# Encoder layer in Strassen-Winograd steps: weight-operand splits moved between VectorE and GpSimd, down-weight sums taken singly, change-overs of the down-projection lengthened

## The chip, the cores and the metric

The kernel runs on one core of one Trainium2 chip. The metric is device time in microseconds (us), from the first to the last instruction of an execution with what lies around it. The core's engines are TensorE (PE: matmuls, PEld: weight loads), VectorE (DVE), ScalarE (ACT), GpSimd (POOL) and SyncE (SP), which here only issues DMAs. Each engine takes its instructions in the order in which they are written; between engines they wait for semaphores.

## What is computed

One layer of a bidirectional encoder, in float32, on 2048 + 1024 tokens of width 1024, with the same weights. First token mixing (input projection, Fourier groups, gating heads, output projection), then channel mixing, of which this text treats:

```
def _channel_mixer(h, w_up, conv_w, conv_b, w_down):
    a = h @ w_up                                   # 1024 -> 2 * 2816
    ap = jnp.pad(a, ((0, 0), (1, 1), (0, 0)))
    a = ap[:, :-2] * conv_w[0] + ap[:, 1:-1] * conv_w[1] + ap[:, 2:] * conv_w[2] + conv_b
    gate, up = a[..., :D_FF], a[..., D_FF:]        # D_FF = 2816
    return (jax.nn.gelu(gate) * up) @ w_down
```

RMSNorm stands before and after each half, and a residual is added.

## The kernel before

**Split products.** A float32 matmul is made of three in a faster format: each operand is split into h (a rounded copy, made by ScalarE) and l (the rest, source minus h, a subtraction of two SBUF tiles of 128x512 by VectorE or GpSimd), and h*h, h*l and l*h are summed in PSUM. `split` (L99) does this for the moving weights of a step, `Stage.prep` (L148) for the operands that stay through a stage.

**Steps and products.** The large projections run as Strassen-Winograd steps: a 2x2 block product done in seven smaller products, from sums of the operands. Class `Step` holds one: `sums` makes four sums of the left operand on GpSimd (s0 to s3 in the profile, L181 to L184), `prep(j)` splits left operand j (tiles w0 to w6), `mm(j)` is one product: 3n matmuls of 128x512, n = 4 in the up-projection, and 3 or 4 in the down-projection. `post(j)` combines the results out of PSUM on VectorE. The seven products are named B11, B21, T4, T2, T3, T1, B22 (indices 0 to 6), and p0 to p6 in the profile are their results.

**Slots.** The order of all work is written out by hand. `at(slot, order, fn)` notes a function for a slot; slots are counted in products of TensorE, and within a slot LOAD comes before PREP, MM, OUT and STORE. At the end all is written in this order. Left operands are split LEAD slots ahead of their product (3 in up-projection blocks 1 and 2, otherwise 2) and loaded 6 slots ahead.

**Up-projection.** Three blocks of 1024 tokens; in each, 22 steps (ft) of seven products. The stage operands x (7 times 4 tiles) stay through a block; `turnover` spreads the loading and splitting of the next block's over slots around the block boundary: it starts `lead` slots before it and spreads 28 tiles over `span` slots. The first two and last two steps of a block run as interleaved pairs. Of a step's seven splits the tuple `POOL` names those that GpSimd makes: (4,), T3 alone (tile w4u). After the products come the convolution (ACT, then VectorE in `taps`), GELU on ACT, and a multiply of 128x1024 on GpSimd (`gate`, L1190, t0u). Block 0 also computes the four sums per step and stores them; blocks 1 and 2 load them (tiles a0 to a6 of the half pool H).

**Down weights.** In block 1 also the four sums of the down-projection's weights are made, for 11 pairs of rows: `wd_load` (four loads), `wd_sums` (four subtractions and sums on GpSimd, L126 to L128 and L694), `wd_store` (four stores), once in 7 slots. They come behind a step's multiply.

**Down-projection.** Three groups q of the inner dimension, n = 3, 4 and 4; in each, 12 steps (tp) of seven products. The stage operands w (weights and their sums, tiles srw, split into sow) stay through a group, and `turnover` changes them with lead 10 and span 14 for q = 0, 6 and 10 for q = 1 and 2. In `Stage.prep` the tiles with even k are split by VectorE, those with odd k by GpSimd.

Of the kernel before, what the change touches and what calls it, by code (L numbers as in the profile page):

```python
# [15 lines left out]
ALU = mybir.AluOpType  # L16
# [17 lines left out]
def tile_trunk(  # L34
# [6 lines left out]
    nc = tc.nc  # L41
# [8 lines left out]
    def half(name, dt=F32, shape=(128, 512)):  # L50
        return H.tile(list(shape), dt, tag="h", name=name)
# [30 lines left out]
    vec = nc.vector  # L82
# [32 lines left out]
    LOAD, PREP, MM, OUT, STORE = range(5)  # L115

    def at(slot, order, fn, *args):
        events[slot].append((order, len(events[slot]), fn, args))
# [3 lines left out]
    B11, B21, T4, T2, T3, T1, B22 = range(7)  # L122

    def right_sums(t1, b11, b12, b21, b22, last=True):

        nc.gpsimd.tensor_tensor(t1, b12, b11, op=ALU.subtract)  # L126
        nc.gpsimd.tensor_tensor(b12, b22, b12, op=ALU.subtract)
        nc.gpsimd.tensor_tensor(b11, b12, b11, op=ALU.add)  # L128
        if last:
            nc.gpsimd.tensor_tensor(b21, b11, b21, op=ALU.subtract)  # L130


    class Stage:
# [14 lines left out]
        def prep(self, j, ks=range(4)):  # L148
            for k in ks:
                if k >= self.n:  # L150
                    return
                r = self.raw[j][k]
                t = unit(f"so{self.name}{j}{k}", F32R, (128, 2, 512))
                nc.scalar.copy(t[:, 0], r)
                eng = vec if k % 2 == 0 or self.name == 'x0' and j in (B11, T2) else nc.gpsimd
                eng.tensor_tensor(t[:, 1], r, t[:, 0].bitcast(F32), op=ALU.subtract)  # L156
                self.raw[j][k] = None
                self.op[j] = (self.op[j] or []) + [t]
# [429 lines left out]
    for pr in range(12):  # L588
        s = SB + 7 * pr
# [97 lines left out]
            nc.sync.dma_start(bs[q], wd[(ka, kb)[q // 2], :, c : c + 512])  # L687
        raws["wd", i] = bs

    def wd_sums(i):  # L690
        t1 = half(f"wt{i}")
        bs = raws["wd", i]
        right_sums(t1, *bs, False)
        nc.gpsimd.tensor_tensor(bs[2], bs[2], bs[0], op=ALU.subtract)  # L694
        bs.append(t1)

    def wd_store(i):
        b11, b12, b21, _, t1 = raws.pop(("wd", i))
# [322 lines left out]
    for i, m in enumerate(mixes):  # L1021
        s = B1 + 4 * i
# [55 lines left out]
    class Up(Step):  # L1078
# [5 lines left out]
        def __init__(self, stage, blk, ft):  # L1084
            super().__init__(stage, f"u{blk}_{ft}")
            self.blk, self.ft, self.t, self.src = blk, ft, {}, {}
            self.LEAD = 3 if blk else 2

        def fetch(self):
            for i in range(2):  # L1090
# [112 lines left out]
    s = B1 + 4 * len(mixes)  # L1203
    for blk in range(3):

        def x_src(j, a, m, dst, blk=blk):
            nc.sync.dma_start(dst[:, :m], xo_d[blk, j, :, a : a + m])

        stage = Stage(f"x{blk}", 4, x_src)
        if blk == 1:  # L1210
            for i in range(NFT // 2):
                at(s + 7 * i + 22, LOAD, wd_load, i)
                at(s + 7 * i + 25, PREP, wd_sums, i)
                at(s + 7 * i + 29, STORE, wd_store, i)
        if blk:
            turnover(s, stage, Up.ORDER, 12, 22)
        else:
            for i, j in enumerate(Up.ORDER):
                d = s + max(2 * i - 3, -2)
                at(d - 1 - (i > 0), LOAD, stage.load, j)  # L1220
                at(d, PREP - 0.3, stage.prep, j)
        for ft in range(NFT):
            u = Up(stage, blk, ft)

            pair = ft < 2 or ft > NFT - 3
            place(s - 7 * (ft % 2) if pair else s, u, ft % 2 if pair else None)
            first = blk == 0 and ft < 2
            if first:
                u.POOL = ()
                at(u.s0 - 2, LOAD, u.load)  # L1230
                at(u.s0 - 2, PREP - 0.2, u.sums)
                products(u)
            elif blk == 0:
                steps(u, 3)
            else:
                for i, j in enumerate(u.ORDER):
                    at(pos(u, i) - 6, LOAD, u.load_left, j)
                products(u)
            if blk == 0:
                at(u.s0 + (4 if pair else 2), STORE, u.sstore)  # L1240
            at(pos(u, 4), OUT + 0.1, u.centre, 1)
            at(pos(u, 4) + 1, OUT + 0.2, u.taps, 1, 0)
            at(pos(u, 4) + 2, OUT + 0.2, u.taps, 1, 1)
            at(pos(u, 6), OUT + 0.1, u.centre, 0)
            at(pos(u, 7), OUT + 0.2, u.taps, 0, 0)
            at(pos(u, 8), OUT + 0.6, u.taps, 0, 1)
            at(pos(u, 10), OUT + 0.3, u.gate)
            at(pos(u, 12), STORE, u.store)
            s += 7
        if blk == 1:  # L1250
            at(s + 5, OUT + 0.5, last_token)
            at(s + 6, STORE, last_token_store)
# [106 lines left out]
    for q in range(3):  # L1359

        def w_src(j, a, m, dst, q=q):
            k0, n = GROUPS[q]
            kk = KPAIRS.index((k0, k0 + n)) + a
            if j in (B11, B21, B22):
                k = k0 + a + (0 if j == B11 else n)
                c = 512 if j == B22 else 0
                src = wd[k : k + m, :, c : c + 512]
            else:
                src = wo_d[(T1, T2, T3, T4).index(j), kk : kk + m]
            nc.sync.dma_start(dst[:, :m], src.rearrange("k p n -> p k n"))  # L1370

        stage = Stage(f"w{q}", GROUPS[q][1], w_src)
        turnover(s, stage, Down.ORDER, *(() if q else (10, 14)))
        if q == 2:
            at(s - 2, LOAD, po_load)
        for tp in range(12):
            d = Down(stage, q, tp)
            place(s, d)
            steps(d, 3)
            if q == 0:  # L1380
                at(s + 8, STORE, d.cstore)
                s += 7
                continue
            at(s - 2, LOAD, d.cload)
            if q == 1:
                at(s + 8, STORE, d.cstore2, 0)
                at(s + 8, STORE, d.cstore2, 1)
            elif tp == 11:
                at(s + 1, LOAD, d.closing_load)
                at(s + 2, OUT + 0.1, d.square, 0, 0)  # L1390
                at(s + 4, OUT + 0.1, d.square, 1, 1)
                at(s + 5, OUT + 0.1, d.square, 0, 1)
                at(s + 6, OUT + 0.1, d.square, 1, 0)
                at(s + 6, OUT + 0.2, d.closing_out)
            else:
                e = 3 if d.closing else 0
                at(s + 10 - e, MM, d.squares)
                at(s + 11 - e, LOAD, d.xload)
                at(s + 11 - e, PREP + 0.5, d.scale)
                at(s + 12 - e, PREP + 0.5, d.yout, 1)  # L1400
                at(s + 14 - e, OUT + 0.3, d.yout, 0)
                at(s + 14 - e, STORE, d.ystore, 1)
                at(s + 15 - e, STORE, d.ystore, 0)
            s += 7
# [121 lines left out]
```

## Time and profile before

| | us |
|---|---|
| median of 3 runs (2756.62 to 2758.92) | 2758.53 |
| the profiled execution | 2759.55 |
| its span, first to last instruction | 2757.6 |
| PE busy | 2650.9 (96%) |
| DVE busy | 2156.4 (78%) |
| ACT busy | 1199.7 (44%) |
| POOL busy | 1172.1 (43%) |

The granted clock of TensorE is 0.986 of full speed on average. A busy time says how long an engine had an instruction in work; it includes time in which the instruction itself was held up. Idle time of an engine other than TensorE costs nothing as long as TensorE does not wait for it.

### The profile page before, as it was taken

What the parts mean: (1) busy time and instruction counts of PE and PEld (TensorE: products, weight loads), DVE (VectorE), ACT (ScalarE), POOL (GpSimd) and SP (SyncE); (2) the same over time, 40 slices, a digit from 0 to 9 for tenths busy, and PEclk for the clock granted to TensorE, in tenths of its full rate; (3) what the DMA queues carried; (4) which work ended last, traced back from release to release, by engine and by line L of the source; (5) the groups of instructions that cost most, each with busy time, mean ns of one, the idle gap of its engine ahead of it and who ended that gap; (6) DMA issues with size and microseconds to landing.
All of it is one profiled execution on the core that took longest, in us unless ns stands there. A gap on an engine that the chain in (4) does not pass through costs nothing.

```text
span 2757.6 us, 35060 instructions
## 1 busy us (share of the span) xinstructions
PE 2650.9 (96%) x11930; PEld 2164.6 (78%) x11930; DVE 2156.4 (78%) x3282; ACT 1199.7 (44%) x2261; POOL 1172.1 (43%) x772
## 2 busy tenths in 40 slices
PE   8899999999889999999999998999998999999998
PEld 7788877887768888877777886888886877887886
DVE  6777756678888788888888888888887567668887
ACT  5445524555544444454333444444444352224333
POOL 3644221235655556643444233222124344326666
PEclk9999999999999999999999999999999999999999
DMA  9223375658934445564665364343353475456665
GB/s 350 104 84 115 122 276 203 228 175 282 334 134 155 155 155 180 180 209 148 217 220 198 129 221 123 107 138 124 117 181 129 131 234 167 160 184 229 206 222 198
DMA packets 323923, 498.08 MB, mean 181 GB/s; under 512 B 27232, under 2 KB 176224, under 8 KB 323744
## 3 DMA queue, kind: packets, MB, share of 16 engines
q1 hardware_dynamic: 323744, 495.85, 54.3%
q8 instruction: 93, 1.52, 0.2%
q14 instruction: 86, 0.70, 0.1%
HBM read 337.42 MB, written 158.35 MB: 180 GB/s over the span
## 4 chain that ended last, share of the span: by engine, by line
PE 43%; DVE 7%; issue 3%; ACT 1%; DMA 1%; POOL 0%; SPq 0%; DVEq 0%; ACTq 0%; POOLq 0%
PE p0d L203 12%; PE p5u L203 4%; PE p4u L203 4%; PE p2u L203 4%; PE p3u L203 4%; PE p6d L203 3%; PE p0u L203 3%; PE p1d L203 3%; PE p5d L203 3%; PE p1u L203 3%; PE p6u L203 2%; DVE sow L156 1%; DVE w3u L101 1%; DVE t1u L1153 1%; DVE t0u L1153 1%
## 5 line engine op out<-in xcount | busy, mean ns | idle before, releaser
L1190 POOL TENSOR_TENSOR t0u<-t0u,t1u 128x1024 f32<-128x1024 f32 x66 | 177.3, 2688 | 424.7 <-ACT t0u L1189 267.2
L203 PE MATMUL p0u<-sox,w0u 128*128 128x512 f32 x792 | 194.6, 394 | 11.7 <-DVE w0u L101 11.6
L203 PE MATMUL p1u<-sox,w1u 128*128 128x512 f32 x792 | 194.3, 392 | 6.8 <-DVE w1u L101 6.6
L203 PE MATMUL p3u<-sox,w3u 128*128 128x512 f32 x792 | 195.2, 393 | 5.7 <-DVE w3u L101 4.9
L203 PE MATMUL p5u<-sox,w5u 128*128 128x512 f32 x792 | 194.0, 392 | 6.2 <-DVE w5u L101 6.2
L203 PE MATMUL p4u<-sox,w4u 128*128 128x512 f32 x792 | 192.7, 392 | 5.5 <-POOL w4u L101 5.0
L203 PE MATMUL p2u<-sox,w2u 128*128 128x512 f32 x792 | 191.9, 392 | 5.1 <-DVE w2u L101 5.1
L203 PE MATMUL p6u<-sox,w6u 128*128 128x512 f32 x792 | 191.1, 391 | 1.2 <-DVE w6u L101 1.2
L203 PEld LDWEIGHTS p0u<-sox,w0u 128*128 128x128 f32 x792 | 149.1, 189 | 47.3 <-DVE w0u L101 16.3
L1141 ACT ACTIVATE t1u<-p2u,cbt,cwt 128x512 f32<-128x512 f32 x66 | 51.5, 780 | 301.1 <-DVE p2u L1129 293.3
L203 PEld LDWEIGHTS p1u<-sox,w1u 128*128 128x128 f32 x792 | 147.2, 188 | 44.3 <-DVE w1u L101 13.3
L203 PEld LDWEIGHTS p3u<-sox,w3u 128*128 128x128 f32 x792 | 146.8, 188 | 43.9 <-DVE w3u L101 11.9
L203 PEld LDWEIGHTS p5u<-sox,w5u 128*128 128x128 f32 x792 | 146.6, 188 | 43.9 <-DVE w5u L101 12.8
L203 PEld LDWEIGHTS p4u<-sox,w4u 128*128 128x128 f32 x792 | 147.1, 188 | 42.5 <-POOL w4u L101 8.5
L203 PEld LDWEIGHTS p2u<-sox,w2u 128*128 128x128 f32 x792 | 149.8, 189 | 37.2 <-DVE w2u L101 5.9
L203 PEld LDWEIGHTS p6u<-sox,w6u 128*128 128x128 f32 x792 | 148.9, 188 | 33.9 <-DVE w6u L101 2.8
L1141 ACT ACTIVATE t0u<-p1u,cbt,cwt 128x512 f32<-128x512 f32 x66 | 51.5, 780 | 256.8 <-DVE p1u L1135 256.8
L1189 ACT ACTIVATE t0u<-t0u 128x1024 f32<-128x1024 f32 x66 | 70.1, 1062 | 171.2 <-DVE t0u L1153 139.3
L181 POOL TENSOR_TENSOR s0d<-ra1d 128x512 f32<-128x512 f32 (+1 forms) x36 | 50.2, 1396 | 204.1 <-DMA ra1d<-g_d 190.1
L93 POOL TENSOR_SCALAR r_v<-ss 128x2 f32<-128x2 f32 (+1 forms) x38 | 15.9, 417 | 261.4 <-ACT scr L894 156.7
L101 POOL TENSOR_TENSOR w4u<-a4u,w4u 128x512 fp32r<-128x512 f32 x44 | 61.3, 1395 | 143.6 <-ACT w4u L100 119.9
L1153 DVE SCALAR_TENSOR_TENSOR t0u<-p6u,cwt,t0u 128x511 f32<-128x511 f32 (+4 forms) x220 | 111.9, 534 | 7.1 <-ACT t0u L1141 2.0
(348 smaller groups left out, 7040.5 us busy)
## 6 DMA issues: line engine op xcount, KB each, us to landing
g_d<-t0u SPq DMA_DIRECT2D x66, 512.0 KB, 2.9
srx<-xo_d SPq DMA_DIRECT2D x42, 512.0 KB, 6.5
xT<-xT SPq DMA_DIRECT2D x24, 512.0 KB, 8.1
xc<-xc SPq DMA_DIRECT2D x24, 512.0 KB, 5.3
zz<-z_d SPq DMA_DIRECT2D x48, 256.0 KB, 5.8
xr<-x_po SPq DMA_DIRECT2D x24, 512.0 KB, 4.9
xo_d<-hT SPq DMA_DIRECT2D x48, 256.0 KB, 3.6
ra0d<-g_d SPq DMA_DIRECT2D x24, 512.0 KB, 4.6
```

The lines of the kernel that those rows point to most:

```text
L93: nc.gpsimd.tensor_scalar(v, ss, 1.0 / n, EPS, op0=ALU.mult, op1=ALU.add)
L101: (eng or vec).tensor_tensor(l, src, h.bitcast(F32), op=ALU.subtract)
L156: eng.tensor_tensor(t[:, 1], r, t[:, 0].bitcast(F32), op=ALU.subtract)
L181: nc.gpsimd.tensor_tensor(s1, a21, a22, op=ALU.add)
L203: nc.tensor.matmul(ps, lhsT=w[:, a, k], rhs=op[k][:, b], start=k == 0 and a + b == 0 and not chained, stop=k == n - 1 and a == 1, skip_gro ...
L1141: nc.scalar.activation(t[:, i], p, AF.Identity, bias=cbt[:, ti : ti + 1], scale=cwt[:, ti, 1:2])
L1153: vec.scalar_tensor_tensor(d, a, w, d, op0=ALU.mult, op1=ALU.add)
L1189: nc.scalar.activation(ga, ga, AF.Gelu_apprx_tanh)
L1190: nc.gpsimd.tensor_tensor(ga, ga, self.t[1], op=ALU.mult)
```

## The change

Four edits:

1. `Stage.prep`: the stage operands w of the down-projection are all split by VectorE (77 splits instead of 42; GpSimd made 35).
2. `wd_sums(i, n)` makes one of the four sums; they stand two slots apart, and a pair of rows comes every 12 slots instead of 7, from slot 10 of block 1 on instead of 22. The store is two slots behind the last sum.
3. In blocks 1 and 2 of the up-projection GpSimd makes three splits of a step, T3, T4 and B21 (w4u, w2u, w1u), instead of T3 alone.
4. The change-overs of the down-projection: lead and span (10, 14) become (14, 18) for q = 0, (6, 10) become (16, 20) for q = 1 and (7, 11) for q = 2.

```diff
-                eng = vec if k % 2 == 0 or self.name == 'x0' and j in (B11, T2) else nc.gpsimd
+                eng = vec if k % 2 == 0 or self.name[0] == 'w' or self.name == 'x0' and j in (B11, T2) else nc.gpsimd
...
-    def wd_sums(i):
-        t1 = half(f"wt{i}")
+    def wd_sums(i, n):
+
         bs = raws["wd", i]
-        right_sums(t1, *bs, False)
-        nc.gpsimd.tensor_tensor(bs[2], bs[2], bs[0], op=ALU.subtract)
-        bs.append(t1)
+        if n == 0:
+            bs.append(half(f"wt{i}"))
+        b11, b12, b21, b22, t1 = bs
+        out, x, y, op = (
+            (t1, b12, b11, ALU.subtract), (b12, b22, b12, ALU.subtract),
+            (b11, b12, b11, ALU.add), (b21, b21, b11, ALU.subtract),
+        )[n]
+        nc.gpsimd.tensor_tensor(out, x, y, op=op)
...
             self.LEAD = 3 if blk else 2
+            if blk:
+                self.POOL = (T3, T4, B21)
...
-                at(s + 7 * i + 22, LOAD, wd_load, i)
-                at(s + 7 * i + 25, PREP, wd_sums, i)
-                at(s + 7 * i + 29, STORE, wd_store, i)
+                d = s + 10 + 12 * i
+                at(d, LOAD, wd_load, i)
+                for n in range(4):
+                    at(d + 3 + 2 * n, PREP, wd_sums, i, n)
+                at(d + 11, STORE, wd_store, i)
...
-        turnover(s, stage, Down.ORDER, *(() if q else (10, 14)))
+        turnover(s, stage, Down.ORDER, *((14, 18), (16, 20), (7, 11))[q])
```

GpSimd's queue in block 1, from the multiply of step 7 on (t0u1_7; w4u1_9 is a split for step 9, wt and wd are sums of down weights). Before:

```order
L1190 TENSOR_TENSOR t0u1_7_12204<-t0u1_7_12204,t1u1_7_12158 128x1024
L126 TENSOR_TENSOR wt5_12315<-wd51_12236,wd50_12235 128x512
L127 TENSOR_TENSOR wd51_12236<-wd53_12238,wd51_12236 128x512
L128 TENSOR_TENSOR wd50_12235<-wd51_12236,wd50_12235 128x512
L694 TENSOR_TENSOR wd52_12237<-wd52_12237,wd50_12235 128x512
L101 TENSOR_TENSOR w4u1_9_12366<-a4u1_9_12291,w4u1_9_12366 128x512
L1190 TENSOR_TENSOR t0u1_8_12383<-t0u1_8_12383,t1u1_8_12337 128x1024
```

The same place now:

```order
L1197 TENSOR_TENSOR t0u1_7_12187<-t0u1_7_12187,t1u1_7_12140 128x1024
L700 TENSOR_TENSOR wt4_12320<-wd41_12247,wd40_12246 128x512
L101 TENSOR_TENSOR w4u1_9_12346<-a4u1_9_12274,w4u1_9_12346 128x512
L700 TENSOR_TENSOR wd41_12247<-wd43_12249,wd41_12247 128x512
L101 TENSOR_TENSOR w2u1_9_12397<-a2u1_9_12318,w2u1_9_12397 128x512
L700 TENSOR_TENSOR wd40_12246<-wd41_12247,wd40_12246 128x512
L101 TENSOR_TENSOR w1u1_9_12442<-a1u1_9_12370,w1u1_9_12442 128x512
L1197 TENSOR_TENSOR t0u1_8_12363<-t0u1_8_12363,t1u1_8_12315 128x1024
L700 TENSOR_TENSOR wd42_12248<-wd42_12248,wd40_12246 128x512
```

The burst of four sums behind the multiply is taken apart; two splits more stand between two multiplies.

VectorE's queue towards the end of group 0 of the down-projection, where the splits of group 1's stage operands begin (sow100: group 1, product B11, tile 0; w5d0_11: step 11 of group 0). Before:

```order
L101 TENSOR_TENSOR w5d0_11_19754<-s0d0_11_19672,w5d0_11_19754 128x384
L156 TENSOR_TENSOR sow100_19757<-srw100_19695,sow100_19757 128x512
L156 TENSOR_TENSOR sow102_19763<-srw102_19697,sow102_19763 128x512
L1307 TENSOR_TENSOR c0d0_11_19746<-c0d0_11_19746,p1d0_11_19766 128x512
L101 TENSOR_TENSOR w4d0_11_19783<-s2d0_11_19674,w4d0_11_19783 128x384
L156 TENSOR_TENSOR sow110_19789<-srw110_19713,sow110_19789 128x512
L101 TENSOR_TENSOR w6d0_11_19810<-s3d0_11_19675,w6d0_11_19810 128x384
L156 TENSOR_TENSOR sow112_19813<-srw112_19729,sow112_19813 128x512
```

Now:

```order
L156 TENSOR_TENSOR sow100_19588<-srw100_19528,sow100_19588 128x512
L156 TENSOR_TENSOR sow101_19591<-srw100_19528,sow101_19591 128x512
L1316 TENSOR_TENSOR c1d0_9_19542<-c1d0_9_19542,p6d0_9_19594 128x512
L101 TENSOR_TENSOR w1d0_10_19607<-ra0d0_10_19506,w1d0_10_19607 128x384
L156 TENSOR_TENSOR sow102_19610<-srw102_19544,sow102_19610 128x512
L101 TENSOR_TENSOR w3d0_10_19626<-s1d0_10_19563,w3d0_10_19626 128x384
L156 TENSOR_TENSOR sow103_19629<-srw102_19544,sow103_19629 128x512
L156 TENSOR_TENSOR sow110_19632<-srw110_19560,sow110_19632 128x512
```

They begin more than a step earlier, and tiles 1 and 3, GpSimd's before, stand in VectorE's queue. At the boundary from the up-projection, ahead of the first split w0d0_0, VectorE's queue holds 15 stage splits of group 0 where it held 8, and the splits w2u and w1u of the last two steps are gone from there.

## Rows read from the trace of the kernel before

**Rows 1.** Page, part 1: busy us, share of the span, instructions of TensorE

```profile
PE 2650.9 (96%) x11930; PEld 2164.6 (78%) x11930; DVE 2156.4 (78%) x3282; ACT 1199.7 (44%) x2261; POOL 1172.1 (43%) x772
```

**Rows 2.** Chain of waits: start us, length us, engine, result, line, matmuls

```profile
1269.86 2.72 PE p0u L203 x12
...
1294.50 2.72 PE p4u L203 x12
...
1502.16 2.72 PE p4u L203 x12
...
1633.07 5.45 PE p2u L203 x24
...
1737.99 2.72 PE p0u L203 x12
...
2042.63 5.44 PE p0u L203 x24
...
2120.49 4.08 PE p0d L203 x18
...
2249.01 4.09 PE p0d L203 x18
...
2295.27 5.44 PE p0d L203 x24
...
2485.67 5.45 PE p0d L203 x24
...
2533.74 5.44 PE p0d L203 x24
```

**Rows 3.** Timeline of TensorE, block 0's last pair: start us, length us, matmuls

```profile
1197.64 3.76 PE L203 MATMUL p1u<-sox,w1u 128*128 128x512 f32 x14
```

**Rows 4.** Windows: start:end, length; busy us (instructions): PE, PEld, DVE, ACT, POOL

```profile
1315.28:1336.06 20.78, 19.95 (x85) 15.45 (x85) 18.05 (x30) 8.05 (x13) 10.11 (x6) 1.00 0.68 215
1757.03:1776.07 19.04, 19.04 (x86) 15.77 (x85) 16.50 (x33) 8.20 (x14) 4.10 (x2) 1.00 0.38 126
2120.49:2134.77 14.28, 14.28 (x64) 11.82 (x64) 7.16 (x12) 5.24 (x11) 4.74 (x5) 1.00 0.41 129
2333.35:2352.39 19.04, 19.04 (x86) 15.77 (x85) 11.99 (x16) 4.36 (x7) 5.81 (x5) 1.00 0.50 165
2571.82:2590.86 19.04, 19.04 (x85) 15.77 (x85) 15.85 (x18) 6.46 (x11) 12.37 (x8) 1.00 0.69 220
```

**Rows 5.** Timelines of GpSimd and VectorE, block 1 (1345) and block 2 (1770)

```profile
1345.02 2.39 POOL L1190 TENSOR_TENSOR t0u<-t0u,t1u 128x1024 f32<-128x1024 f32 x1 [10.43 <-ACT t0u L1189]
...
1345.21 2.75 DVE L101 TENSOR_TENSOR w1u<-a1u,w1u 128x512 fp32r<-128x512 f32 x1
...
1770.98 0.68 DVE L101 TENSOR_TENSOR w1u<-a1u,w1u 128x512 fp32r<-128x512 f32 x1
```

**Rows 6.** Groups by line: busy us, mean ns of one, idle before and its releaser

```profile
L101 POOL TENSOR_TENSOR w4u<-a4u,w4u 128x512 fp32r<-128x512 f32 x44 | 61.3, 1395 | 143.6 <-ACT w4u L100 119.9 <-PE p3u L203 13.1 <-PE p0u L203 10.6
L156 DVE TENSOR_TENSOR sow<-srw,sow 128x512 fp32r<-128x512 f32 x42 | 58.9, 1415 | 0.3 <-ACT sow L154 0.3
L101 DVE TENSOR_TENSOR w1u<-a1u,w1u 128x512 fp32r<-128x512 f32 x44 | 54.6, 1241 | 9.0 <-ACT w1u L100 4.5 <-issue 4.3
```

**Rows 7.** Waits of TensorE (us, times, longest): block 1; first down step; whole span

```profile
PE p3u L203 <- DVE w3u L101: 4.9, 10, 0.5
...
PE p0d L203 <- DVE w0d L101: 3.9, 1, 3.9
...
PE p4u L203 <- POOL w4u L101: 5.0, 8, 0.6
```

**Rows 8.** Timelines of GpSimd and VectorE, change-over from group 0 to 1

```profile
2267.98 16.90 POOL L156 TENSOR_TENSOR sow<-srw,sow 128x512 fp32r<-128x512 f32 x10
...
2272.47 1.18 DVE L101 TENSOR_TENSOR w1d<-ra0d,w1d 128x512 fp32r<-128x512 f32 x1
2273.57 3.48 DVE L156 TENSOR_TENSOR sow<-srw,sow 128x512 fp32r<-128x512 f32 x2
```

## The prediction

> **What bounds the kernel now.** Read part 1 of the page first: TensorE is busy in 2650.9 us [rows 1], so a gain can come only out of the remainder and out of stretches where its products run at half clock or wait. Next the chain of waits. It is nearly all matmuls, and the start times of products show where the pace is lost. A product of the up-projection is twelve matmuls and takes 2.72 us [rows 2]; seven make a step of 19.04 us, which block 2 and the second group of the down-projection (n = 4) hold exactly, and a step of the first group (n = 3) takes 14.28 us, 2.04 a product [rows 4]. From one start to a later one, less what the products in between need, gives the loss of each stretch (starts from [rows 2], but for one):
>
> - Into block 1: from 1197.64 [rows 3] to 1269.86 [rows 2] are 72.22 us for 23 products, 62.56 us. Lost 9.7.
> - Block 1, ten steps: 1294.50 to 1502.16 [rows 2], 207.66 us for 190.4. Lost 17.3. These are the steps with down-weight sums.
> - Block 1 to block 2: 1633.07 to 1737.99, 104.92 us for 34 products, 92.48. Lost 12.4.
> - Block 2 to the down-projection: 2042.63 to 2120.49, 77.86 us for 14 products of 2.72 and 13 of 2.04, 64.6. Lost 13.3.
> - Group 0 to 1: 2249.01 to 2295.27, 46.26 us for 8 products of 2.04 and 6 of 2.72, 32.6. Lost 13.6.
> - Group 1 to 2: 2485.67 to 2533.74, 48.07 us for two steps, 38.08. Lost 10.0.
>
> Together 76.3 us, all that this change can reach. Then the waits of TensorE: behind these losses stand splits (the second halves of operands), nearly all VectorE's; in block 1 ten waits for w3u, and 3.9 us for the first w0d of the down-projection [rows 7].
>
> Last the timelines of VectorE and GpSimd, for why the splits are late. A split by VectorE alone takes 0.68 us (w1u in block 2). In block 1 the same split starts at 1345.21, 0.19 us behind a GpSimd multiply that runs to 1347.41, and takes 2.75 us: it ends only after that multiply [rows 5]. Where both engines split at the same time, ten GpSimd splits take 16.90 us and two VectorE splits 3.48 us, so each pair of splits costs about 1.7 us, and even a step's own split takes 1.18 [rows 8]. VectorE alone would do those two splits in 1.36. VectorE instructions on two SBUF tiles and GpSimd instructions thus take turns here; **the turns are the scarce thing**, not either engine's busy share.
>
> **The change part by part, against the profiled execution's 2759.55 us.**
>
> *Sums of down weights, block 1.* The window of a step with sums holds GpSimd 10.11 us in 6 instructions, block 2's 4.10 in 2 [rows 4]; the difference, 6.0 us, is one burst of four sums directly behind the multiply, once in each 7 slots. Now they come singly, two slots apart, once in 12 slots: 3.5 us per step on average. Two splits of 1.395 each [rows 6] come on top: 4.1 + 3.5 + 2.8 = 10.4 us of GpSimd in a step, as much as before, but nowhere six instructions in a row. VectorE loses two splits, 1.36 us at 0.68 and more at the 1.241 that w1u averages [rows 6]: from 18.05 of 20.78 us it comes to about 16.5 or less, which is what block 2 carries without loss [rows 4]. What was late was w3u, by at most 0.5 us [rows 7], behind the chain w1u, posts, ScalarE's conv, w3u; w1u now leaves that chain. GpSimd's new splits follow ScalarE's casts, when it sits idle (4.10 of 19.04 us busy). The order also shows the loads less tightly bound to freed half tiles. A single sum can still hold one VectorE split, but 2.75 less 0.68 bounds it at 2.1 us, and the chain is shorter by a split. Bounds: gain 8 to 17. I take **15.5**, nearest to block 2's steady row.
>
> *Three splits of seven on GpSimd, block 2.* The step is already at 19.04; GpSimd goes from 4.10 to 6.9 us. Gain 0. If its cover fails, w2u or w1u is late (a rival below).
>
> *Into block 1, and block 1 to 2.* Two splits per step leave VectorE, and the alternating stage splits (x) stay as they are. But the two multiplies that hold VectorE there also stay, and GpSimd's new splits queue behind them. Per step the exchange is 0.7 to 1.2 us of VectorE twice against 1.4 of GpSimd twice. For the first transition block 0's last steps are unchanged: -1.5 to 3, I take **1.5** of 9.7. For the second: 0 to 6, I take **3** of 12.4.
>
> *Stage splits of the down weights on VectorE, longer change-overs.* 77 splits: before, 42 on VectorE at 1.415 us on average [rows 6] and 35 on GpSimd. Now 77 on VectorE, which at 0.68 is 52.4 us against 59.4: less VectorE time for more work, if GpSimd stays out of the way. It keeps the four left sums of each step (4.74 us a step of 14.28, [rows 4]); each may hold a VectorE split for up to 1.74 - 0.68 = 1.06 us [rows 8].
>
> Group 0 to 1: 28 splits over 20 slots, 16 of 2.04 and 4 of 2.72 us. VectorE's room: 2.04 - 7.16/7 = 1.02 in each of the first, 2.72 - 11.99/7 = 1.01 in the others [rows 4]; 20.3 us. Work: 28 x 0.68 = 19.0, and 11 sums at 0 to 1.06 each, I take 6. Overflow 4.7. The same sum for before: room 10 slots, 10.2; work 14 x 1.74 = 24.4 and ten of the steps' splits at 0.5 more, 5; overflow 19.2, of which 13.6 was lost, so that 5.6 was absorbed by operands prepared ahead. By that nothing need be left now; I leave 3, since ScalarE's casts stand in between. Gain 8 to 13.6, taken **10.5**.
>
> Group 1 to 2: 28 splits over 11 slots, one more than before. Room 7 x 1.01 + 4 x (2.72 - 15.85/7) = 8.9. Work 19.0 and about 4 for six sums; overflow 14. Before: room 7.9, work 29.4, overflow 21.5, lost 10.0, absorbed 11.5. Left between 14 - 11.5 = 2.5 and 14 - 5.6 = 8.4. Gain 1.6 to 7.5; taken **6**, since absorption belongs to the place. Here VectorE is loaded beyond its room still.
>
> Block 2 to group 0: ahead of the first w0d, VectorE's order holds 8 stage splits before and 15 now, and four splits of the last two steps fewer: 3 x 0.68 = 2.0 us more in front of the very instruction that TensorE waited 3.9 us for [rows 7]. Against it four earlier slots with 2.72 - 16.50/7 = 0.36 of room each, 1.4 us, and GpSimd's stage splits gone. Bounds -3 to 6, taken **2** of 13.3.
>
> *Loads, stores, queues.* The bytes are the same. SP now issues the four weight loads and stores of a sum every 12 slots instead of 7; the store stands two slots behind the last sum (before four), so SP can wait there for GpSimd, with the a loads queued behind it. These loads run three slots, 8.2 us, ahead of their casts, which covers a wait of a slot or two; cost 0 to 3, in the range.
>
> Sum: 15.5 + 1.5 + 3 + 10.5 + 6 + 2 = 38.5. 2759.55 - 38.5 = 2721; the median of the runs lies 1 us under the profiled one, so **2720 us**. Own range, from the terms' bounds (not all at one end): 2704 to 2738.
>
> **The Trainium skill** speaks against the up-projection part: GPSIMD Engine Reference, section 4.1 Engine selection, sends elementwise work on a tile to VectorE, GPSIMD being about twice as slow with two inputs. This trace agrees on size: 1395 against 680 ns. By that rule alone 88 moved splits would be a loss of 63 us of engine time (an estimate from it); whether any of it is TensorE's time the rule does not say. Its section 1 Specifications calls the SBUF interfaces shared with VectorE where that one reads two SBUF inputs; the 2.75 us of w1u agrees.
>
> **The rivals.**
>
> (a) *The turns in block 1 stay as scarce.* The GpSimd time of a step there is the same 10.4 us, each instruction still holds a VectorE split that meets it, and only who is held changes. Then block 1 gains 4 rather than 15.5: 2732 us. For: equal GpSimd time. Against: turns fall from 10.1 + 6 x 0.68 = 14.2 of 20.78 to 10.4 + 4 x 0.68 = 13.1, and the burst is gone.
>
> (b) *GpSimd becomes the late one in the up-projection.* In-order behind multiplies that wait for ScalarE's GELU, its splits w4u, w2u, w1u come after TensorE wants them. The price is in the waits: p4u waited for GpSimd eight times, 0.6 us at most [rows 7]. Once a step in blocks 1 and 2, 44 x 0.6 = 26: 2746 us. Against: it sits idle for 15 of 19 us in block 2, and the new splits are placed ahead of the multiply.
>
> (c) *Slower: VectorE is overloaded in the change-overs.* If its splits keep 1.415 us each, since the left sums and multiplies still take turns, 35 more cost 49.5 us, against 10 x 1.02 + 1.0 + 1.4 = 12.6 of added room: 36.9 us more at three transitions, less the 20 gained in the up-projection: 2759.5 + 16.9, 2775 us. It decides from a mean at which 77 splits cost 59.4 + 12.6 + 20 = 92 us, 1.19 us each. For: at group 1 to 2 the splits exceed the room even uncontended. Against: 14 of every 28 stage splits, GpSimd's, no longer compete.
>
> That the edit would not do what it says is excluded by the order: every stage split of w is in VectorE's queue, the sums stand singly.
>
> **How the numbers follow.** Forecast 0.62, (a) 0.14, (b) 0.12, (c) 0.08, and 0.04 for more than counted (one more transition emptied, 2700). The range 2703 to 2744 takes the forecast with its bounds, (a) and most of (b), and leaves out about 0.18. A measurement here tells about 0.2%, 5.5 us, from no change. Faster than 2753: forecast, (a), the upper case and most of (b), 0.88; slower than 2764: (c), 0.08; the same 0.04.
>
> **What would show it.** Right: block 1's steps at 19.04 to 19.3 us and no wait for w3u there; VectorE's stage splits of w under 0.9 us on average, GpSimd without any; group 0 to 1 losing under 4 us, group 1 to 2 under 5, and the first w0d still late by some us. Wrong: waits of TensorE for GpSimd's w2u or w1u in most steps (b); block 1's steps still near 20.8 (a); stage splits of w above 1.2 us (c).

## The result, and the profile after

The changed kernel takes 2716.76 us (median of 4 runs, 2715.09 to 2717.41) against 2757.9 us before (4 runs, 2756.62 to 2758.92): the ratio is 0.985, with a 95% interval from 0.9833 to 0.9867. 2720 us were predicted. The sum came out; three of its six terms did not stay within their bounds: into block 1 and block 1 came out above them (block 1 by 0.6 us, with eleven steps in the row below where the prediction took ten), block 2 to group 0 below.

Part 1 of the page of after, the line that answers to [rows 1] (busy us, share of the span, instructions):

```profile
PE 2630.0 (97%) x11930; PEld 2166.6 (80%) x11930; DVE 2080.6 (77%) x3229; ACT 1200.0 (44%) x2261; POOL 1217.7 (45%) x825
```

VectorE is busy for 76 us less, with 53 instructions fewer (88 splits of the up-projection gone, 35 stage splits come). At 0.68 each that is 36 us: the rest is time in which its instructions had been held up. GpSimd has 46 us more.

The windows of after, one row for each stretch of the prediction, each cut between the starts of two products, the same two in every kernel (start:end, length, busy us and instructions of PE, PEld, DVE, ACT, POOL, then TensorE's clock, the DMA share and GB/s):

```profile
1196.90:1265.02 68.12, 64.52 (x277) 51.37 (x277) 60.90 (x96) 36.52 (x64) 40.49 (x25) 1.00 0.44 142
1289.50:1498.94 209.44, 209.44 (x925) 173.48 (x924) 171.56 (x304) 91.33 (x149) 104.79 (x70) 1.00 0.59 193
1610.46:1709.46 99.00, 95.02 (x409) 77.50 (x408) 85.63 (x155) 49.37 (x83) 46.20 (x29) 0.98 0.48 148
2014.10:2097.86 83.76, 72.40 (x295) 57.56 (x294) 71.29 (x124) 38.64 (x70) 35.10 (x25) 0.92 0.44 141
2226.38:2260.40 34.02, 33.62 (x148) 27.52 (x147) 31.80 (x43) 20.08 (x39) 15.24 (x10) 1.00 0.94 306
2450.80:2493.64 42.84, 38.88 (x169) 31.28 (x168) 42.12 (x58) 25.71 (x45) 14.94 (x8) 1.00 0.85 285
```

From each length goes what its products need (2.72 us each with n = 4, 2.04 with n = 3): 23 products, 62.56; 77, 209.44; 34, 92.48; 14 and 14, 66.64; 7 and 7, 33.32; 14, 38.08. What is left is lost. Second row: eleven steps of block 1 are now 19.04 us each to the hundredth. The fourth row is the only one that got worse, and the only one with a clock well under full speed.

| lost, us | before | after | gain | predicted gain (bounds) |
|---|---|---|---|---|
| into block 1 | 9.5 | 5.6 | 3.9 | 1.5 (-1.5 to 3) |
| block 1 | 17.6 | 0.0 | 17.6 | 15.5 (8 to 17) |
| block 1 to 2 | 12.4 | 6.5 | 5.9 | 3 (0 to 6) |
| block 2 to group 0 | 13.3 | 17.1 | -3.9 | 2 (-3 to 6) |
| group 0 to 1 | 13.6 | 0.7 | 12.9 | 10.5 (8 to 13.6) |
| group 1 to 2 | 10.0 | 4.8 | 5.2 | 6 (1.6 to 7.5) |
| sum | 76.4 | 34.7 | 41.7 | 38.5 |

The spans differ by 42.7 us; nearly all of it is in these six stretches. Groups by line of after, to be held against [rows 6] (busy us, mean ns of one, idle before):

```profile
L156 DVE TENSOR_TENSOR sow<-srw,sow 128x512 fp32r<-128x512 f32 x77 | 67.1, 902 | 3.1 <-ACT sow L154 3.1
L101 POOL TENSOR_TENSOR w2u<-a2u,w2u 128x512 fp32r<-128x512 f32 x44 | 60.7, 1382 | 157.5 <-ACT w2u L100 147.5 <-PE p4u L203 5.1 <-DMA wd<-wd 4.9
L101 POOL TENSOR_TENSOR w1u<-a1u,w1u 128x512 fp32r<-128x512 f32 x44 | 57.5, 1308 | 32.3 <-ACT w1u L100 22.5 <-issue 9.9
```

77 stage splits take VectorE 67.1 us, where 42 took 58.9. GpSimd's new splits waited for ScalarE, and TensorE waits for none of them.

The change from group 0 to 1 shows it best. The groups of stage splits in that stretch before, VectorE's half and GpSimd's; columns as above:

```profile
L156 DVE TENSOR_TENSOR sow<-srw,sow 128x512 fp32r<-128x512 f32 x14 | 23.1, 1663 | 0.3 <-ACT sow L154 0.3
L156 POOL TENSOR_TENSOR sow<-srw,sow 128x512 fp32r<-128x512 f32 x14 | 23.0, 1675 | 21.4 <-ACT sow L154 21.4
```

The same groups in after, where there is only VectorE's:

```profile
L156 DVE TENSOR_TENSOR sow<-srw,sow 128x512 fp32r<-128x512 f32 x28 | 23.4, 858 | 0.0
```

28 splits by VectorE alone cost it as much time as 14 with GpSimd beside it: in the short change-over of before, GpSimd's half of the work had saved VectorE nothing. With the longer one this does not hold; the run e3_alternate below has that pair.

### The profile page after: what moved, and what is told of

Read it like the earlier page. It is cut to its first block, busy times and chain, and to the rows that moved or that the text cites. A ratio compares the mean times of both kernels' runs of the same rounds, so it can differ in the third digit from the quotient of the medians.

```text
span 2714.9 us, 35070 instructions
## 1 busy us (share of the span) xinstructions
PE 2630.0 (97%) x11930; PEld 2166.6 (80%) x11930; DVE 2080.6 (77%) x3229; ACT 1200.0 (44%) x2261; POOL 1217.7 (45%) x825
## 5 line engine op out<-in xcount | busy, mean ns | idle before, releaser
L1197 POOL TENSOR_TENSOR t0u<-t0u,t1u 128x1024 f32<-128x1024 f32 x66 | 167.8, 2543 | 164.1 <-ACT t0u L1196 157.9
L203 PEld LDWEIGHTS p0u<-sox,w0u 128*128 128x128 f32 x792 | 149.3, 189 | 42.5 <-DVE w0u L101 11.5
L101 POOL TENSOR_TENSOR w2u<-a2u,w2u 128x512 fp32r<-128x512 f32 x44 | 60.7, 1382 | 157.5 <-ACT w2u L100 147.5
```

Of the source, the lines that this page charges most:

```text
L101: (eng or vec).tensor_tensor(l, src, h.bitcast(F32), op=ALU.subtract)
L203: nc.tensor.matmul(ps, lhsT=w[:, a, k], rhs=op[k][:, b], start=k == 0 and a + b == 0 and not chained, stop=k == n - 1 and a == 1, skip_gro ...
L1197: nc.gpsimd.tensor_tensor(ga, ga, self.t[1], op=ALU.mult)
```

## The experiments

All kernels start from the changed one. The table gives what each loses in the six stretches, worked out as above; "-" means that the stretch stays within 0.7 us of after's. The times of after, g3_both and g4_blocks_too are medians of 4, 4 and 5 runs, the others are single executions; the stretches are those of the profiled execution. The scatter of a single execution is told at the end, so stretches are compared, not totals alone.

| kernel | time, us | into block 1 | block 1 | block 1 to 2 | block 2 to group 0 | group 0 to 1 | group 1 to 2 |
|---|---|---|---|---|---|---|---|
| after | 2716.76 | 5.6 | 0.0 | 6.5 | 17.1 | 0.7 | 4.8 |
| e1_burst | 2724.75 | - | 4.2 | - | - | - | 9.3 |
| e2_one_split | 2724.98 | 9.9 | - | 11.5 | 17.9 | - | - |
| e3_alternate | 2717.57 | - | - | - | 12.2 | 3.6 | 9.7 |
| e4_short_turn | 2730.72 | - | - | - | - | 11.1 | 10.2 |
| f1_group0_alternate | 2711.57 | - | - | - | 12.3 | - | - |
| f2_first_split_early | 2718.55 | - | - | - | 18.5 | - | - |
| f4_no_left_sums | 2711.24 | - | - | 7.6 | - | - | 0.0 |
| f6_w5u_early | 2714.37 | 6.9 | - | 4.7 | - | - | 3.9 |
| g1_group0_gpsimd | 2705.92 | - | - | 7.3 | 6.2 | - | - |
| g2_sums_early | 2707.55 | - | - | - | 12.2 | - | 2.0 |
| g3_both | 2702.32 | - | - | - | 6.2 | - | 1.9 |
| g4_blocks_too | 2700.16 | 3.5 | - | 5.3 | 6.3 | - | 1.9 |

### Each part undone

**The burst of sums** back in block 1:

```diff
-                d = s + 10 + 12 * i
-                at(d, LOAD, wd_load, i)
-                for n in range(4):
-                    at(d + 3 + 2 * n, PREP, wd_sums, i, n)
-                at(d + 11, STORE, wd_store, i)
+                at(s + 7 * i + 22, LOAD, wd_load, i)
+                at(s + 7 * i + 25, PREP, wd_sums, i)
+                at(s + 7 * i + 29, STORE, wd_store, i)
```

> The changed kernel with the four down-weight sums of a pair of rows taken in one burst again, once in 7 slots. Theory of turns (a two-operand VectorE split that meets a GpSimd instruction is held, so six and more GpSimd instructions in a row make operands late): in block 1 GpSimd has 4.1 + 6.0 + 2.8 = 12.9 us a step, the burst stands again in front of the splits w2u and w1u, and the ten steps from 1294 lose 6 to 17 us against 0.0 now: 2723 to 2734 us in all. Rival theory of load (it was VectorE's 18.05 us of 20.78 that bound the step, and taking two splits off it was the cure): VectorE stays near 16.5 us a step, block 1 keeps 19.04 us a step, 2717 us.

**One split of a step** on GpSimd in blocks 1 and 2:

```diff
-                self.POOL = (T3, T4, B21)
+                self.POOL = (T3,)
```

> The changed kernel with one split of a step on GpSimd in blocks 1 and 2 (T3), as before; the sums stay single. Theory of turns: a single sum holds one VectorE split by at most 2.1 us, which the three slots of lead cover; block 1's ten steps lose 0 to 5 us. The two change-overs of the up-projection lose again what they lost before, 9.5 and 12.4 us against 5.6 and 6.5: 2727 to 2732 us in all, and the start of the down-projection keeps its 17.1 or loses more, since w1u is VectorE's again just there. Theory of load: block 1's steps are back at 18.05 us of VectorE and lose up to 17 us: 2740 to 2745 us.

Measured: block 1 loses 4.2 us with the burst and 0.0 with single sums, whoever makes the splits. The window of block 1's eleven steps with the burst (columns as in the windows above):

```profile
1288.96:1502.64 213.68, 212.91 (x926) 171.98 (x924) 184.12 (x299) 89.21 (x145) 127.33 (x84) 1.00 0.69 228
```

The same window with single sums and one split:

```profile
1292.08:1501.52 209.44, 209.44 (x926) 173.42 (x924) 175.13 (x327) 92.27 (x150) 81.04 (x47) 1.00 0.59 193
```

Load as the cause falls: with 327 instructions VectorE is busy for 175 us, with 299 and the burst for 184. Turns came out, but smaller than stated (of the 8 us more of e1_burst 4.6 are lost from group 1 to 2, which the last section takes up): where VectorE has the two splits fewer, the burst costs 4.2 us, not 6 or more. Before, both came together, for 17.6. So spreading the sums alone (singly, and over 12 slots a pair of rows instead of 7) cures block 1, and moving the splits alone would have cured three quarters of it. The moved splits earn their place elsewhere: at the two block changes (9.9 and 11.5 lost without them, against 5.6 and 6.5) and by 0.8 at the start of the down-projection.

The edit of e1_burst brings back the rate of the sums as well as their burst (GpSimd is busy for 127.3 us in the eleven steps, in after for 104.8), and the two were not tried apart. Its loss stands in no wait that the profile lists for a matmul of block 1: in ten of the eleven steps the weight loads of p6u wait for VectorE's split w6u, 5.0 us in all. One of them:

```profile
1394.73 2.14 PEld L203 LDWEIGHTS p6u<-sox,w6u 128*128 128x128 f32 x10 [0.52 <-DVE w6u L101]
```

Before, it was not w3u alone that was late in block 1, as the prediction has it, but also the moved split w1u itself:

```profile
PE p1u L203 <- DVE w1u L101: 3.2, 10, 0.3
```

**Stage splits in turn** again, with the long change-overs, and **short change-overs** with all splits on VectorE:

```diff
-                eng = vec if k % 2 == 0 or self.name[0] == 'w' or self.name == 'x0' and j in (B11, T2) else nc.gpsimd
+                eng = vec if k % 2 == 0 or self.name == 'x0' and j in (B11, T2) else nc.gpsimd
```

> The changed kernel with the stage splits of the down weights taken in turn by VectorE and GpSimd, as before; the long change-overs stay. Theory of turns: 14 pairs at 1.74 us and eleven of the steps' own splits at 0.5 more are 30 us for 20.3 us of room at the change from group 0 to 1; 9.7 over, of which 5.6 was absorbed before: 4 us lost against 0.7. At the change from group 1 to 2 it is 24.4 + 5 for 8.9, 11.5 absorbed: 9 lost against 4.8. Stage splits of VectorE at 1.3 us or more on average. In all 2717 + 3.3 + 4.2 = 2724 us, less up to 4 if the start of the down-projection gets back to its 13.3. Theory of load: half of the 77 splits off VectorE can only help, and the length of the change-over did it all: 2710 to 2717 us.

```diff
-        turnover(s, stage, Down.ORDER, *((14, 18), (16, 20), (7, 11))[q])
+        turnover(s, stage, Down.ORDER, *(() if q else (10, 14)))
```

> The changed kernel with the change-overs of the down-projection as long as before (lead and span 10 and 14, then 6 and 10); all their splits stay with VectorE. Theory of turns: group 0 to 1 has 10.2 us of room for 28 x 0.68 and three for sums, 22; 12 over, 5.6 absorbed: 6 lost against 0.7. Group 1 to 2 hardly changes (lead 6 against 7), 5 to 7 lost. In all 2722 to 2725 us, less up to 4 if the shorter change-over brings the start of the down-projection back to 13.3. Rival: all on VectorE without more room is worse than in turn, group 0 to 1 loses 13.6 or more as before and group 1 to 2 over 10: 2735 us.

Group 0 to 1 lost 13.6 before; the longer change-over alone leaves 3.6, VectorE alone 11.1, both 0.7. Length is the larger part, and neither does without the other. With splits in turn the stated 4 and 9 came out as 3.6 and 9.7, and VectorE's stage splits average 1.28 us. The 30 us of VectorE's work behind the stated 4 did not come out. From group 0 to 1, with the long change-over:

```profile
L156 POOL TENSOR_TENSOR sow<-srw,sow 128x512 fp32r<-128x512 f32 x14 | 20.6, 1480 | 24.8 <-ACT sow L154 24.8
L156 DVE TENSOR_TENSOR sow<-srw,sow 128x512 fp32r<-128x512 f32 x14 | 15.7, 1122 | 2.5 <-ACT sow L154 2.5
```

14 splits take VectorE 15.7 us where 28 alone took 23.4, so here GpSimd's half does save it 7.7 us; the steps' own 28 splits in the same products give 3.5 of that back (24.3 us against 20.8). That TensorE loses 2.9 us more all the same is a matter of when a split is held, not of VectorE's sum: TensorE's longest wait, 1.5 us, ends 0.15 us behind a post of VectorE that stood behind two splits of 1.78 and 1.77 us.

For the short change-over 6 were stated for group 0 to 1, and 13.6 by the rival; 11.1 lies between. From group 1 to 2 its 10.2 are what the rival said (over 10), not the 5 to 7 stated. At the start of the down-projection the old length loses 16.9, the new one 17.1: length does nothing there. The stage splits of e4_short_turn from group 0 to 1:

```profile
L156 DVE TENSOR_TENSOR sow<-srw,sow 128x512 fp32r<-128x512 f32 x28 | 24.2, 914 | 0.0
```

They take 24.2 us, not the 22 taken, and only 2.9 of the overflow was absorbed (24.2 - 10.2 of room = 14.0 over, 11.1 lost), not the 5.6 carried over from before. At the start of the down-projection, splits in turn are better by 4.9 us: there the edit did harm.

### Why the start of the down-projection got worse

VectorE's timeline there, after: start us, length us, instruction, and in brackets the idle time ahead and what ended it. p2u is the post of the last two steps of block 2, w0d the split TensorE waits for.

```profile
2041.21 0.68 DVE L1136 TENSOR_TENSOR p2u<-ru,p2u 128x512 f32<-128x512 f32 x1
2044.43 1.37 DVE L156 TENSOR_TENSOR sow<-srw,sow 128x512 fp32r<-128x512 f32 x1 [2.54 <-ACT sow L154]
2045.72 0.68 DVE L1136 TENSOR_TENSOR p2u<-ru,p2u 128x512 f32<-128x512 f32 x1
...
2048.95 2.80 DVE L156 TENSOR_TENSOR sow<-srw,sow 128x512 fp32r<-128x512 f32 x2 [0.60 <-ACT sow L154]
...
2059.30 0.55 DVE L101 TENSOR_TENSOR w0d<-ra0d,w0d 128x384 fp32r<-128x384 f32 x1
```

The same place before:

```profile
2068.33 0.68 DVE L1129 TENSOR_TENSOR p2u<-ru,p2u 128x512 f32<-128x512 f32 x1
2071.04 0.69 DVE L101 TENSOR_TENSOR w1u<-a1u,w1u 128x512 fp32r<-128x512 f32 x1 [2.02 <-ACT w1u L100]
...
2084.44 0.55 DVE L101 TENSOR_TENSOR w0d<-ra0d,w0d 128x384 fp32r<-128x384 f32 x1
```

From the first post to w0d it was 16.1 us and is 18.1, and the first post begins 5.24 us after TensorE's product p2u began, where it was 4.10. Together these are the 3.1 us by which the wait for w0d grew (3.9 to 7.0). Before, VectorE waited there once, for the cast of w1u. That split is GpSimd's now, but stage splits stand in its place, and VectorE waits for their casts, between two posts. ScalarE's timeline in after says why:

```profile
2041.93 0.78 ACT L1148 ACTIVATE t1u<-p2u,cbt,cwt 128x512 f32<-128x512 f32 x1 [9.63 <-DVE p2u L1136]
2042.61 0.77 ACT L1148 ACTIVATE t1u<-p5u,cbt,cwt 128x512 f32<-128x512 f32 x1
2043.27 0.61 ACT L100 CAST w1u<-a1u 128x512 fp32r<-128x512 f32 x1
2043.78 0.62 ACT L154 CAST sow<-srw 128x512 fp32r<-128x512 f32 x1
```

The cast for the split stands behind a conv that waits for VectorE's first post, and the second post stands behind the split: VectorE waits for ScalarE, which waited for VectorE. The same splits meet GpSimd's w1u and left sums (1.37, and 2.80 for two).

**The late split moved alone:**

```diff
-            at(pos(step, i) - step.LEAD, PREP, step.prep, j)
+            at(pos(step, i) - (5 if i == 0 and step.nm == 'd0_0' else step.LEAD), PREP, step.prep, j)
```

> The changed kernel with one split moved: w0d of the down-projection's first step stands five slots ahead of its product instead of two, in front of five groups of taps on VectorE. TensorE waited 7.0 us for it. Theory of the single place (this split is late because of where it stands): the start of the down-projection loses 10 to 11 us instead of 17.1, 2710 us. Theory of the backlog (VectorE has more to do there than fits, whatever the order, and the next splits w1d, w3d, w5d stand behind the same taps): the 7 us turn up as a wait for w1d, the loss stays at 15 to 18 us, 2715 to 2717 us.

Backlog: the 7.0 us for w0d are gone, and the next product waits instead, since ScalarE's cast for it comes behind convs that wait for VectorE's posts. 18.5 are lost, a little over the 15 to 18 stated. From the waits of TensorE (us, times, longest):

```profile
PE p1d L203 <- ACT w1d L100: 8.1, 1, 8.1
```

**Group 0 alone in turn, then mostly on GpSimd:**

```diff
-                eng = vec if k % 2 == 0 or self.name[0] == 'w' or self.name == 'x0' and j in (B11, T2) else nc.gpsimd
+                eng = vec if k % 2 == 0 or self.name in ('w1', 'w2') or self.name == 'x0' and j in (B11, T2) else nc.gpsimd
```

> The changed kernel with the stage splits of group 0 alone taken in turn by VectorE and GpSimd; groups 1 and 2 stay with VectorE. Theory (each change-over for itself: where VectorE is behind and GpSimd idle for ten us at a time, splits on GpSimd help; where GpSimd has the left sums of the down-projection, they harm): the start of the down-projection loses 12.2 us as in the run with all three groups in turn, against 17.1; the change from group 0 to 1 stays at 0.7, from 1 to 2 at 4.8; 2712 us. Rival (GpSimd's splits of group 0 gave 5 us there only because of where the whole queue stood, or are lost again at the next change): 2716 to 2721 us.

```diff
-                eng = vec if k % 2 == 0 or self.name[0] == 'w' or self.name == 'x0' and j in (B11, T2) else nc.gpsimd
+                pool = k % 2 or self.name == 'w0' and j in (T1, T3, B22)
+                eng = vec if not pool or self.name in ('w1', 'w2') or self.name == 'x0' and j in (B11, T2) else nc.gpsimd
```

> Like f1_group0_alternate (group 0 in turn), and GpSimd also takes all tiles of T1, T3 and B22 of group 0, which stand on VectorE between the last posts and taps of block 2. There VectorE waited 2.6 + 0.65 us for ScalarE's cast of a stage operand, whose turn came after a conv that waited for VectorE's own post, and six stage splits took 6.5 us ahead of the posts that everything behind them waits for. GpSimd is idle there. Theory of the backlog (any VectorE time taken away ahead of those posts moves TensorE's products forward one for one): 6 to 8 us less in VectorE's queue, the start of the down-projection loses 5 to 7 us instead of 12.3; 2705 us. Rival (GpSimd's splits come late there, behind w1u and the left sums, or hold VectorE's other splits): 11 to 15 lost, 2710 to 2714 us.

Both as the theory had them: 12.3, then 6.2 lost. VectorE's timeline in g1_group0_gpsimd:

```profile
2037.86 0.69 DVE L1137 TENSOR_TENSOR p2u<-ru,p2u 128x512 f32<-128x512 f32 x1
2040.57 0.70 DVE L1137 TENSOR_TENSOR p2u<-ru,p2u 128x512 f32<-128x512 f32 x1 [2.02 <-PE p2u L204]
...
2050.34 1.31 DVE L101 TENSOR_TENSOR w0d<-ra0d,w0d 128x384 fp32r<-128x384 f32 x1
```

12.5 us from post to w0d, and the only wait left is one for TensorE itself. The taps between them read PSUM, and GpSimd beside them does not hold them: each row of five takes 2.03 us here, as in after.

### Why the change from group 1 to 2 still loses

```diff
-        at(pos(step, -ahead), PREP - 0.2, step.sums)
+        at(pos(step, -ahead), PREP - 0.2, step.no_sums if step.nm in ('d2_0', 'd2_1') else step.sums)
```

> The changed kernel with the four left sums (s0 to s3, GpSimd) of the first two steps of group 2 left out; the products take unsummed operands in their place. Everything else, VectorE's work included, stays. Theory of turns (the stage splits meet GpSimd's sums there and are held to 1.2 to 1.75 us): without the sums they take 0.6 to 0.7 us each, and the change from group 1 to 2 loses 1 to 2.5 us instead of 4.8; 2713 to 2715 us. Theory of load (28 splits at 0.68 are 19 us for 8.9 us of room, the sums do not matter): 4 to 5 us lost as now, 2716 to 2717 us.

Turns, and more than stated: nothing is lost. The window of the change, without those sums:

```profile
2450.06:2488.14 38.08, 38.08 (x170) 31.53 (x168) 35.25 (x58) 24.78 (x44) 0.00 (x0) 1.00 0.93 315
```

The same 58 instructions of VectorE as in after's last row, 35.3 us busy instead of 42.1; eight GpSimd sums had cost it 6.9. This is the cleanest run on turns: VectorE's order is untouched. The sums themselves could have been late too, as ScalarE's casts of summed operands wait for them; but TensorE's longest wait there in after is for one of VectorE's posts, behind stage splits that were held. That wait, and the three splits ahead of it in after and in f4_no_left_sums:

```profile
PE p0d L203 <- DVE c1d L1316: 2.2, 1, 2.2
...
2460.63 4.09 DVE L156 TENSOR_TENSOR sow<-srw,sow 128x512 fp32r<-128x512 f32 x3
...
2459.89 1.89 DVE L156 TENSOR_TENSOR sow<-srw,sow 128x512 fp32r<-128x512 f32 x3
```

The prediction's sum for this place, 19.0 us of splits for 8.9 of room, is refuted as a measure of loss: without the sums VectorE is busy for 35.3 of 38.1 us, and nothing is late.

**The first step's sums earlier** (with group 0 in turn):

```diff
+            if q == 2 and tp == 0:
+                at(s - 11, LOAD - 0.5, d.load)
+                at(s - 9, PREP - 0.2, d.sums)
+                products(d)
+            else:
+                steps(d, 3)
```

> Like f1_group0_alternate, and for the first step of group 2 the rows are loaded 11 slots ahead instead of 6 and its left sums stand 9 slots ahead instead of 3, before the stage splits of group 2 begin. The second step's sums stay where they are. Theory of turns: the four sums of the first step held VectorE's splits by about 4 us; the change from group 1 to 2 loses 0 to 2 us instead of 4.8; 2707 to 2709 us. Rival: the early rows take buffers that the stage loads wait for, the stage splits come later, and 4 to 8 us are lost: 2711 to 2715 us.

2.0 lost, as stated. The sums now run where VectorE has no stage splits.

### The changes between blocks

```diff
+                if ft < 2:
+                    u.EARLY = {T1: 5}
                 for i, j in enumerate(u.ORDER):
-                    at(pos(u, i) - 6, LOAD, u.load_left, j)
+                    at(pos(u, i) - (8 if j in u.EARLY else 6), LOAD, u.load_left, j)
```

> The changed kernel with one split of the first two steps of blocks 1 and 2 moved: w5u stands five slots ahead of its product instead of three, and its load eight instead of six. TensorE waited 3.8 us for it at the change to block 2 (5.2 us with the half clock behind it). Single place: that change loses 2 to 3 us instead of 6.5, the change to block 1 4 instead of 5.6; 2711 us. Backlog: the next splits w2u and w6u are late instead, or the cast for it waits for its load; 0 to 2 us in all, 2715 to 2717 us.

Mostly backlog: 1.8 us gained at block 2, 1.3 lost at block 1. With w5u in time, TensorE waits at block 2 for GpSimd's w2u, 1.8 us, and for w6u.

**Both repairs, then the same for the blocks:**

> The changed kernel with both repairs: T1, T3, B22 and the odd tiles of group 0 split by GpSimd, and the first step of group 2 loaded and summed early. Each stretch for itself: start of the down-projection 6.2 lost, group 0 to 1 about 1, group 1 to 2 2.0; 2702.5 to 2704 us. Rival: the early rows of group 2, or the other queue order, upset a neighbour: 2706 us or more.

```diff
+                pool = k % 2 or self.name == 'w0' and j in (T1, T3, B22) or self.name in ('x1', 'x2') and j in (T3, T1)
```

> g3_both, and in the two change-overs of the up-projection GpSimd also takes all tiles of T3 and T1 of the stage operands x, which stand on VectorE between the last posts and taps of a block (a wait of 3.1 us for ScalarE's cast of one of them, as at the start of the down-projection). Theory of the backlog: the change to block 2 loses 3 to 5 us instead of 6.5, to block 1 4 instead of 5.6; 2699 to 2702 us. Rival: here GpSimd is not idle, it has three splits of each step and the multiplies, so its stage splits hold VectorE's or come late themselves: 5 to 9 and 5 to 7 lost, 2703 to 2707 us.

The repairs add up. g3_both takes 2702.32 us (4 runs, 2700.65 to 2703.8; ratio to before 0.9799, interval 0.9785 to 0.9812), g4_blocks_too 2700.16 (5 runs, 2697.57 to 2701.92; 0.9788, 0.9775 to 0.9801). Both beat the changed kernel. Between the two the runs overlap; the block changes lose 8.8 instead of 12.1 in the profiled executions (3.5 and 5.3, where 4 and 3 to 5 were stated), of which the medians show 2.2.

## Why the prediction was right, and where it was not

- **What bounds.** The reading held: the gain came out of the six stretches, and turns between the two engines made VectorE late (block 1 with and without the burst, group 1 to 2 without the sums). In block 1 it was short: it names w3u as the late split, and w1u was late as often.
- **Sums, block 1.** 15.5 taken, 17.6 measured: the whole loss. Just above the bound of 17. The working gave the moved splits a share that they do not need; e2_one_split loses nothing here.
- **Block changes.** 1.5 and 3 taken, 3.9 and 5.9 measured, the first beyond its upper bound. The term was mis-sized where it called the swap nearly even: e2_one_split puts the two splits at 4.4 and 5.0. It did not weigh that the splits' place in VectorE's queue is ahead of posts and taps; that this is what made them dear was not tested by itself.
- **Block 2 to group 0.** This step failed: 2 taken, -3.9 measured, below the lower bound. It counted 2.0 us more of splits ahead of w0d against 1.4 of room and GpSimd's splits gone. It left out that VectorE would wait for ScalarE's casts (2.54 and 0.60 us against one wait of 2.0 before) and that w1u, now GpSimd's, and the left sums would hold the stage splits there. e3_alternate and f1_group0_alternate lay 4.9 us of it on the edit to `Stage.prep`; e2_one_split shows that the moved splits help by 0.8. The four earlier slots, counted at 1.4 us, gave nothing (16.9 without them in e4_short_turn).
- **Group 0 to 1.** 10.5 taken, 12.9 measured, inside the bounds. The account of room, work and overflow pointed the right way, but its absorbed part is not a constant of the place: 5.6 before, 2.9 in e4_short_turn. Nor is its price of a split one: the 1.74 us for each split in turn are near the 1.66 measured in the short change-over, but with the long one 14 of them take 15.7 us, 1.12 each, so that the 3.6 us of e3_alternate agree with the stated 4 by luck.
- **Group 1 to 2.** 6 taken, 5.2 measured. Right in size, and partly by chance, as the last section tells.
- **The rivals.** (a) fell: block 1 loses nothing. (b) fell: TensorE waits for no w2u or w1u of GpSimd's in after. (c) fell: the mean is 0.902 us, below its 1.19, though just above the 0.9 named as the sign of being right.

So 2720 against 2716.76 is in part luck, a sum in which errors of +2.1 to +2.9 in four terms met -5.9 and -0.8 in two.

The Trainium skill, GPSIMD Engine Reference, section 4.1 Engine selection, sends such splits to VectorE. The runs agree at the change from group 0 to 1 (3.6 us lost in turn, 0.7 without GpSimd) and differ at the start of the down-projection, where seven and then thirteen splits taken from VectorE brought 17.1 down to 12.3 and 6.2; the measurement decides, place by place.

## What to carry to other kernels

Before giving work to an idle engine, ask in each stretch whether its instructions meet two-SBUF instructions of VectorE or ones that read PSUM: in these traces the first paid for it (1.2 to 1.8 us a split instead of 0.68), the second did not (2.03 us a row of taps either way). An instruction that waits on another engine's queue costs the whole queue behind it, so keep operands prepared ahead out of the places where two engines hand results back and forth. Moving one late instruction forward tells a backlog from a bad place: if the wait reappears one product later, take work away instead.

## What the runs showed of the hardware

**Who comes first can decide for several instructions.** After the sums of block 1, e1_burst has the same order in every queue as the changed kernel, yet loses 9.3 us from group 1 to 2 instead of 4.8. GpSimd, VectorE and TensorE at the second step's sums, timelines of after:

```profile
2481.19 3.25 POOL L181 TENSOR_TENSOR s0d<-ra1d 128x512 f32<-128x512 f32 x1 [13.61 <-DMA ra1d<-g_d]
...
2480.79 0.68 DVE L101 TENSOR_TENSOR w4d<-s2d,w4d 128x512 fp32r<-128x512 f32 x1
2481.39 1.89 DVE L156 TENSOR_TENSOR sow<-srw,sow 128x512 fp32r<-128x512 f32 x3
2483.19 0.68 DVE L1316 TENSOR_TENSOR c0d<-c0d,p0d 128x512 f32<-128x512 f32 x1
...
2481.43 2.88 PE L203 MATMUL p5d<-sow,w5d 128*128 128x512 f32 x12
```

The same of e1_burst:

```profile
2484.11 1.30 POOL L181 TENSOR_TENSOR s0d<-ra1d 128x512 f32<-128x512 f32 x1 [13.12 <-DMA ra1d<-g_d]
...
2485.88 5.12 DVE L156 TENSOR_TENSOR sow<-srw,sow 128x512 fp32r<-128x512 f32 x3
...
2484.83 2.88 PE L203 MATMUL p5d<-sow,w5d 128*128 128x512 f32 x12
```

In after the sum starts 0.24 us ahead of TensorE's product p5d, while VectorE is within a split; three more go through at 0.63 each, and the sum takes 3.25 us (1.30 in e1_burst): it ends only after VectorE's next instruction on PSUM has begun. In e1_burst the rows land earlier, the sum starts 0.72 us ahead of p5d and is first, and then three splits take 5.12 us, 1.71 each, a sum in between each time. Turns are thus not strictly alternating: a row of VectorE's splits kept GpSimd out. e4_short_turn has one of each, a row of three at 0.63 each with a sum of 3.02 us beside it, and then a row of three in 5.11 us. What else decides it was not tried. In four other kernels with these queues here (e2_one_split, f1_group0_alternate, f2_first_split_early, g1_group0_gpsimd) 4.8 us are lost as in after, but the 5.2 us gained hang on half a microsecond.

The Trainium skill, SBUF — State Buffer, section SBUF: two separate sides, says that whoever starts first has the shared ports for its whole instruction. The 1.71 us agree; that the held engine stays out over several instructions goes beyond it.

**The part ahead of the stretches is not constant.** Block 0's first product begins at 745.04 us in g3_both and at 749.58 in g4_blocks_too, with nothing changed before it. A few microseconds of a single total say little. A stretch between two products that no edit touches repeats to 0.1 us in most runs, though block 1 to 2 came out 0.8 and 1.1 us longer in g1_group0_gpsimd and f4_no_left_sums, group 0 to 1 by 0.6 in four runs, and group 1 to 2 came out 0.9 shorter in f6_w5u_early.
